# A two-layer decoder trunk (Mamba-2, then sliding-window attention): group 1's transposes one block later, another place for x1, and a last norm that uses TensorE and two store queues

## The chip, the cores and the metric

One core of one Trainium2 chip runs the whole kernel. The metric is the device time of one execution in microseconds (us); the kernel before was timed three times. A profile of one of its executions was taken. Engines: TensorE (PE, matrix products; PEld are its weight loads), VectorE (DVE), ScalarE (ACT), GpSimd (POOL), and SyncE (SP), which here only issues DMAs.

## The reference

The input x has 256 tokens of 2048 numbers, in float32. Two layers follow, each of the form x <- LayerNorm(ALPHA * x + mixer(x)).

The first mixer is a Mamba-2 SSD layer. A projection gives z, xs, B, C and dt. xs, B and C pass a causal convolution of four taps and SiLU. There are 64 heads of width 64 in 8 groups; each group has its own B and C of 128 states. Cut to what matters:

```
zxbcdt = x @ w_in                       # 2048 -> 4096 (z) + 4096 (xs) + 2*1024 (B, C) + 64 (dt)
xbc    = silu(causal_conv(xbc) + conv_b)
y      = ssd(xs * dt, decay(dt * a), B, C) + xs * d_skip
y      = groupwise_rmsnorm(y * silu(z)) * norm_w
x1     = layernorm(ALPHA * x + y @ w_out)
```

The second mixer is grouped-query attention in a window of 128 tokens, with partial rotary positions, a sink per head and a SiLU gate. Keys and values are projected once from x1:

```
kv   = x1 @ kv_w + kv_b
q, g = x1 @ b_w_in                      # 2048 + 2048 columns
o    = softmax_with_sink(rope(q) k^T) v * silu(g)
out  = layernorm(ALPHA * x1 + o @ b_w_out)
```

The layer norm is (x - mean) * rsqrt(var + eps) * g + b, along the 2048 numbers of a token.

## The kernel before

**Precision and weights.** Products run on TensorE in a reduced float32 format. To keep accuracy each operand is split into a high part (a copy, by ACT) and a low part (the difference, by DVE), and three products are added: high*high, high*low, low*high. All weights come from HBM in units of 128 x 2048 float32. `load_unit` (line 101) issues two DMAs of 512 KB on SP's queue into five raw buffers `wr`, has ACT write the high half `wh` (line 112) and DVE the low half `wl` (line 113); there are four `wh` and four `wl` buffers. `next_unit` (line 166) loads two units ahead of their use.

**The first layer.** `group(g)` (line 468) goes through the eight groups. A group consists of ten blocks; a block (`gemm_ws`, line 247) multiplies one unit of weights, stationary, with x, moving (`xH`, `xL`), 48 matmuls of 256 columns (lines 182 to 184). In group 1 and later the blocks are B, C, xs0 to xs3, z0 to z3. The result of an xs block is convolved and passed through SiLU on ACT and DVE (`conv_silu`; the last step is line 322). Later steps of the group are:
- `cb`: products of C and B (lines 390, 391), a mask, and the product with the decay factors `e` (line 395);
- `tr(g, i)`: two transposes of xs_i on TensorE (line 403), and a product with dt on DVE (`xd`, line 408);
- `ymm(g, i)`: the products of `e` and `xd` (line 424) and the skip (line 429);
- `gate(g, i)`: products with z on POOL (lines 436 to 442), a high part on ACT (line 450), a low part on DVE (line 451);
- `norm(g)`: the group's mean square (line 460) and its inverse root on ACT (lines 464, 465).

The out products of group g-1 (`out_unit`, lines 220 to 222, 12 matmuls of 512 columns for each half of the tokens) stand between the blocks of group g. In them y is stationary and the weights move.

**What sets the order.** A table `plan` (built with `at(t, fn, ...)`) says after which block a step is written; t counts blocks, ten to a group. Group 1 has its own entry, with `tr` 4 blocks after the group's start for i = 0, 1; `ymm` for i = 0, 1 and `tr` for i = 2, 3 follow two blocks later, `ymm` for i = 2, 3 four blocks later, and `norm` stands at 10. The framework then places each engine's instructions by its own estimate, so that the order in which an engine gets them is near to the written order but not equal to it.

**Placement in memory.** `xr` holds ALPHA * x and becomes the residual; it lies at the upper end of each partition (16 KiB). Below it, `x1H` and `x1L` (16 KiB each) hold the split output of the first layer; after the last layer's projections are done, the same place holds the tables g and b of the last norm (`gb2`). `x1H` began at byte 180192 of a partition, 480 past a multiple of 512. `xH` begins at 123968 (64 past), `yH`, `yL`, `oH`, `oL`, `wh` and `wl` at multiples of 512.

**The second layer.** For keys, values and queries x1 is stationary and the weights move in 512 columns (`x_stat`, lines 669 to 671: 480 matmuls). For the gate the weights are stationary and x1 moves in 256 columns (lines 182 to 184, called from `gate_block`: 768 matmuls).

**The end.** `out_last` adds the last out products, first all of half 0 of the tokens, then half 1, and takes the statistics of each 512 columns with them (lines 229 and 597). `done2(h)` is the last norm: mean and variance (line 601), the inverse root on ACT (lines 603, 604); then for each of four column ranges t = (x - mean) * g on DVE (line 860). For the ranges in `OFFLOAD` (all four of half 0, ranges 0 and 2 of half 1) ACT multiplies with the inverse root (line 864) and POOL adds b (line 865); for the others DVE does both in one instruction (line 867). SP issues the eight stores (line 868).

Of the kernel before, what the change touches and what calls it, by code (L numbers as in the profile page):

```python
# [8 lines left out]
F32 = mybir.dt.float32  # L9
F32R = mybir.dt.float32r  # L10
I32 = mybir.dt.int32
AF = mybir.ActivationFunctionType
ALU = mybir.AluOpType
AX = mybir.AxisListType

P = 128
S = 256
D = 2048
# [9 lines left out]
TD, TS, CB0, TR0, Y0, CB1 = 5, 5, 8, 9, 10, 5  # L28
# [2 lines left out]
FIRST = [(0, 2), (2, 4), (4, 6), (6, 9), (9, 12), (12, 16)]  # L31
ZPRI = 200
PRE = 1
OFFLOAD = [(0, 1, 2, 3), (0, 2)]
CPRI = 0
OUT_AT = [[], [6, 7, 8, 9]] + [[3, 5, 7, 9]] * 5 + [[7]]

# [22 lines left out]
def trunk(ctx: ExitStack, tc: tile.TileContext, A: dict, out: bass.AP, dbg=None):  # L60
    nc = tc.nc
    PSUM = bass.MemoryType.PSUM

    def pool(name, bufs=1, side=None, space=None, stack=ctx):
        kw = {"space": space} if space is not None else {}
        return stack.enter_context(
            tc.tile_pool(name=name, bufs=bufs, side=side, reuse_waits="tile", **kw)
        )
# [9 lines left out]
    def nm(s):  # L78
        uid[0] += 1
        return f"{s}_{uid[0]}"  # L80
# [4 lines left out]
    def ax_tile():  # L85
        return ax_ps.tile([P, 512], F32, tag="ax", name=nm("ax"), bufs=4)

    cc = cst.tile([P, 896], F32, tag="cc", name="cc")
    ident = cc[:, 0:128]
    ones = cc[:, 128:256]  # L90
# [113 lines left out]


    xp = pool("xp", side="right")
    xr = xp.tile([P, 2, D], F32, tag="xr", name="xr")
    a_stack = ExitStack()
    yp = pool("yp", stack=a_stack)
    w_stack = ExitStack()  # L210
# [330 lines left out]
    def at(t, fn, *a):  # L541
        plan.setdefault(t, []).append((fn, *a))

    at(35, rotary)
    for g in range(NG):
        t = 10 * g
        n = 1 if g == 0 else 0
        if g == 0:
            at(TD, turn_dt, *dts)
            at(TS, sum_decay, 0, 0)  # L550
            at(TS, load_decay, 0, 1)
            at(TS + 1, sum_decay, 0, 1)
            at(TS + 1, exp_decay, 0, 0)
            at(TS + 1, exp_decay, 0, 1)
            pos = dict(cb=CB0, tr=TR0, z=0, norm=Y0 + 5)
        elif g == 1:
            at(Y0, load_decay, 1, 0)
            at(Y0 + 2, sum_decay, 1, 0)
            at(Y0 + 2, load_decay, 1, 1)
            at(Y0 + 4, sum_decay, 1, 1)  # L560
            at(Y0 + 5, exp_decay, 1, 0)
            at(Y0 + 5, exp_decay, 1, 1)
            pos = dict(z=6, cb=CB1, tr=4, norm=10)
        else:
            at(t - 5, load_decay, g, 0)
            at(t - 3, sum_decay, g, 0)
            at(t - 3, load_decay, g, 1)
            at(t - 1, sum_decay, g, 1)
            at(t, exp_decay, g, 0)
            at(t, exp_decay, g, 1)  # L570
            pos = dict(z=6, cb=CB_AT, tr=TR_AT, norm=NORM_AT)
        at(t + pos["cb"], cb, g)

        at(t + pos["tr"], tr, g, 0)
        at(t + pos["tr"], tr, g, 1)
        for k in range(2):
            for i in (2 * k, 2 * k + 1):
                at(t + pos["tr"] + 2 + 2 * k, ymm, g, i)
            if k == 0:
                at(t + pos["tr"] + 2, tr, g, 2)  # L580
                at(t + pos["tr"] + 2, tr, g, 3)
        for i in range(4):
            at(t + max(pos["tr"] + 2 + 2 * (i // 2), pos["z"] + i), gate, g, i)
        at(t + pos["norm"], norm, g)
# [14 lines left out]
    def norm_scale(lp, st, h):  # L599
        mv = lp.tile([P, 2], F32, tag="mv", name=nm("mv"), bufs=2)  # L600
        nc.vector.bn_aggr(mv[:], st[:, h, :, :])
        rs = lp.tile([P, 1], F32, tag="rs", name=nm("rs"), bufs=2)
        nc.scalar.activation(rs[:], mv[:, 1:2], AF.Ln, bias=eps_t[:])
        nc.scalar.activation(rs[:], rs[:], AF.Exp, scale=-0.5)
        return mv, rs
# [35 lines left out]
    bp = pool("bp")  # L641
# [207 lines left out]
    gb2 = [gp.tile([P, D], F32, tag=f"gb{i}", name=f"gb2_{i}") for i in range(2)]  # L849
# [3 lines left out]

    def done2(h):
        mv, rs = norm_scale(bp, st2, h)
        for c in range(4):
            sl = slice(c * 512, (c + 1) * 512)
            v = xr[:, h, sl]
            t = bp.tile([P, 512], F32, tag="pt", name=nm("t"), bufs=4)
            nc.vector.scalar_tensor_tensor(  # L860
                t[:], v, mv[:, 0:1], gb2[0][:, sl], ALU.subtract, ALU.mult
            )
            if c in OFFLOAD[h]:
                nc.scalar.activation(t[:], t[:], AF.Copy, scale=rs[:])
                nc.gpsimd.tensor_tensor(v, t[:], gb2[1][:, sl], ALU.add)
            else:
                nc.vector.scalar_tensor_tensor(v, t[:], rs[:], gb2[1][:, sl], ALU.mult, ALU.add)  # L867
            nc.sync.dma_start(out[h * P : (h + 1) * P, sl], v)

    if PRE:  # L870
        tc.keep_in_program_order(nc.scalar.preload_act_table_set("natural_log_exp_and_others"))
    out_last(*os_[3], None, lambda h, nb: norm_stats(st2, h, nb), done2)


# [87 lines left out]
```

## Time and profile before

| | |
|---|---|
| median of three runs | 1046.5 us (1046.29 to 1047.47) |
| profiled execution, its own time | 1046.29 us |
| span of the profiled execution | 1044.5 us |
| TensorE busy | 1019.1 us, 98% |
| DVE, ACT, POOL busy | 810.5, 518.4, 104.2 us |
| mean granted TensorE clock | 0.992 |
| DMA | 203.50 MB, 195 GB/s on the mean |

How to read the rows: a row of a timeline begins with the start and the duration in us, then the engine, the line of the kernel, the operation, what is written and read, the shape, and the count where neighbours of one kind are merged; a bracket at the end gives the idle time of the engine before the row, and what ended it. A row of a group has the count, the busy time, the mean duration of one in ns and the idle time before them. A row of stretches has the length, the busy time of PE, PEld, DVE, ACT and POOL (with counts), the granted clock, the DMA share and GB/s. Ends of matmuls are modelled, so that a rate is read from one start to the next.

### The profile page before, as it was taken

The numbers are of one execution on the slowest core, as the hardware profiler recorded it, in microseconds if no ns is written. First come the engines' busy times: TensorE is split into PE (matmuls) and PEld (weight loads), VectorE is DVE, ScalarE is ACT, GpSimd is POOL, SyncE is SP. The second block draws the span as 40 slices with busy tenths as digits, with TensorE's granted clock in tenths as the row PEclk, the third lists the DMA queues.
The fourth block names the chain that finished last, engine by engine and source line by source line (L and its number), as shares of the span: only waits on it lengthen the run. The fifth ranks groups of instructions, "written<-read, shape, count | busy, mean of one in ns | idle before, by whom it ended". The sixth has DMA issues, their size and how long they took to land. (4 is left out here: it accounts for less than half of the span.)

```text
span 1044.5 us, 17586 instructions
## 1 busy us (share of the span) xinstructions
PE 1019.1 (98%) x7020; PEld 920.8 (88%) x7020; DVE 810.5 (78%) x1212; ACT 518.4 (50%) x770; POOL 104.2 (10%) x114
## 2 busy tenths in 40 slices
PE   6999899999999999999999999999999999999995
PEld 6999789999999999999999999877887978978974
DVE  5899997876888778787788786698576775775777
ACT  6664545444645544544544464434464544543631
POOL 0001221012003002102102202201000000000003
PEclk9999899999999999999999999999999999999998
DMA  8885586466566655756656555736645455455532
GB/s 277 317 301 198 179 270 226 165 201 215 182 202 226 216 182 195 229 183 208 217 182 207 183 168 176 269 123 224 205 142 172 140 182 165 145 176 179 176 111 80
DMA packets 57170, 203.50 MB, mean 195 GB/s; under 512 B 6448, under 2 KB 8000, under 8 KB 56320
## 3 DMA queue, kind: packets, MB, share of 16 engines
q1 hardware_dynamic: 56016, 196.86, 56.6%
q0 software_dynamic: 1072, 5.53, 1.6%
q8 instruction: 55, 0.90, 0.3%
q14 instruction: 27, 0.22, 0.1%
HBM read 200.13 MB, written 2.23 MB: 194 GB/s over the span
## 5 line engine op out<-in xcount | busy, mean ns | idle before, releaser
L112 ACT ACTIVATE wh<-wr 128x1024 fp32r<-128x1024 f32 x326 | 337.9, 1054 | 324.0 <-PE mm L183 130.1
L113 DVE TENSOR_TENSOR wl<-wr,wh 128x1024 fp32r<-128x1024 f32 x326 | 394.8, 1224 | 103.4 <-ACT wh L112 102.2
L182 PE MATMUL mm<-xH,wh 128*128 128x256 f32 x1296 | 367.9, 284 | 7.2 <-ACT xH L141 6.2
L184 PE MATMUL mm<-xH,wl 128*128 128x256 f32 x1296 | 363.7, 281 | 0.5 <-DVE wl L113 0.4
L183 PE MATMUL mm<-xL,wh 128*128 128x256 f32 x1296 | 363.6, 281 | 0.2 <-DVE xL L142 0.2
L182 PEld LDWEIGHTS mm<-xH,wh 128*128 128x128 f32 x1296 | 245.5, 190 | 10.1 <-ACT xH L141 6.4
L184 PEld LDWEIGHTS mm<-xH,wl 128*128 128x128 f32 x1296 | 245.9, 190 | 0.9 <-DVE wl L113 0.6
L183 PEld LDWEIGHTS mm<-xL,wh 128*128 128x128 f32 x1296 | 245.0, 189 | 1.4 <-DVE xL L142 0.4
L220 PE MATMUL mm<-wh,yH 128*128 128x512 f32 x256 | 101.0, 394 | 0.0
L222 PE MATMUL mm<-wl,yH 128*128 128x512 f32 x256 | 99.9, 390 | 0.0
L221 PE MATMUL mm<-wh,yL 128*128 128x512 f32 x256 | 99.8, 390 | 0.0
L436 POOL TENSOR_TENSOR yz<-yz,z 128x256 f32<-128x256 f32 x32 | 37.3, 1165 | 530.0 <-DVE z L383 469.2
L182 PE MATMUL mm<-x1H,wh 128*128 128x256 f32 x256 | 73.2, 286 | 0.0
L183 PE MATMUL mm<-x1L,wh 128*128 128x256 f32 x256 | 71.9, 281 | 0.0
L184 PE MATMUL mm<-x1H,wl 128*128 128x256 f32 x256 | 71.9, 281 | 0.0
L318 DVE SCALAR_TENSOR_TENSOR cv<-mm,pc,cv 128x255 f32<-128x255 f32 x144 | 68.6, 476 | 1.9 <-ACT cv L316 0.7
L669 PE MATMUL mm<-wh,x1H 128*128 128x512 f32 x160 | 64.1, 400 | 0.0
L671 PE MATMUL mm<-wl,x1H 128*128 128x512 f32 x160 | 63.5, 397 | 0.2
L670 PE MATMUL mm<-wh,x1L 128*128 128x512 f32 x160 | 63.4, 396 | 0.2 <-DVE x1L L633 0.2
L222 PEld LDWEIGHTS mm<-wl,yH 128*128 128x128 f32 x256 | 48.0, 188 | 10.5
L220 PEld LDWEIGHTS mm<-wh,yH 128*128 128x128 f32 x256 | 48.1, 188 | 9.2 <-DVE yz L429 0.2
L221 PEld LDWEIGHTS mm<-wh,yL 128*128 128x128 f32 x256 | 48.1, 188 | 9.1
(173 smaller groups left out, 1316.5 us busy)
## 6 DMA issues: line engine op xcount, KB each, us to landing
wr<-in_wa SPq DMA_DIRECT2D x158, 512.0 KB, 5.0
wr<-in_wo SPq DMA_DIRECT2D x64, 512.0 KB, 4.4
rb<-rscr SPq DMA_DIRECT2D x32, 512.0 KB, 4.7
wr<-in_wq SPq DMA_DIRECT2D x32, 512.0 KB, 4.3
wr<-in_wg SPq DMA_DIRECT2D x32, 512.0 KB, 4.7
wr<-in_wb SPq DMA_DIRECT2D x32, 512.0 KB, 4.3
wr<-in_wkv SPq DMA_DIRECT2D x8, 512.0 KB, 4.9
xr<-in_xk SPq DMA_DIRECT2D x2, 1024.0 KB, 9.7
```

Of the source, the lines that this page charges most:

```text
L112: nc.scalar.activation(hi[:, sl], raws[c][:], AF.Copy)
L113: nc.vector.tensor_tensor(lo[:, sl], raws[c][:], hi[:, sl].bitcast(F32), ALU.subtract)
L182: nc.tensor.matmul(ps, ah, bh, start=first, stop=False)
L183: nc.tensor.matmul(ps, ah, bl, start=False, stop=False)
L184: nc.tensor.matmul(ps, al, bh, start=False, stop=last)
L220: nc.tensor.matmul(ps[:], aH[:, k, hs], u.h[:, ks], start=k == 0, stop=False)
L221: nc.tensor.matmul(ps[:], aL[:, k, hs], u.h[:, ks], start=False, stop=False)
L222: nc.tensor.matmul(ps[:], aH[:, k, hs], u.l[:, ks], start=False, stop=k == 3)
L318: nc.vector.scalar_tensor_tensor(a[:, sft:], ps[:, : S - sft], w(3 - sft), a[:, sft:], ALU.mult, ALU.add)
L669: nc.tensor.matmul(ps[:], x1H[:, kk, hs], u.h[:, ks], start=kk == 0, stop=False)
L670: nc.tensor.matmul(ps[:], x1L[:, kk, hs], u.h[:, ks], start=False, stop=False)
L671: nc.tensor.matmul(ps[:], x1H[:, kk, hs], u.l[:, ks], start=False, stop=kk == KT - 1)
```

## The change

Three things change. In group 1, `tr` and what follows from it, and `norm`, move one block later in the plan. The tile `xr` gets 104 more numbers per partition that nobody uses, so that what lies below it moves down by 416 bytes; `x1H` then begins at byte 179776, 64 past a multiple of 512. The last norm's half 0 does all four ranges with ACT and POOL, as before; half 1 is written anew: for ranges 0 and 1 TensorE first adds b (a product of a row of ones with b) into PSUM, then multiplies t with a diagonal matrix `dg` of the inverse roots, ACT copies the sum out of PSUM and issues the store on its own queue; ranges 2 and 3 are done by DVE and stored by SP. POOL has no part in half 1.

```
-OFFLOAD = [(0, 1, 2, 3), (0, 2)]
...
-    xr = xp.tile([P, 2, D], F32, tag="xr", name="xr")
+    xr = xp.tile([P, 2 * D + 104], F32, tag="xr", name="xr")[:, : 2 * D].rearrange("p (h d) -> p h d", h=2)
...
-            pos = dict(z=6, cb=CB1, tr=4, norm=10)
+            pos = dict(z=6, cb=CB1, tr=5, norm=11)
...
     def done2(h):
         mv, rs = norm_scale(bp, st2, h)
+        if h:
+            dg = bp.tile([P, P], F32, tag="dg", name="dg")
+            pss = [ax_tile(), ax_tile()]
+            for c in range(2):
+                sl = slice(c * 512, (c + 1) * 512)
+                nc.tensor.matmul(pss[c][:], ones[0:1, :], gb2[1][0:1, sl], start=True, stop=False)
+            nc.scalar.activation(dg[:], ident, AF.Copy, scale=rs[:])
+            for c in range(4):
+                sl = slice(c * 512, (c + 1) * 512)
+                v = xr[:, h, sl]
+                o = out[h * P : (h + 1) * P, sl]
+                t = bp.tile([P, 512], F32, tag="pt", name=nm("t"), bufs=4)
+                nc.vector.scalar_tensor_tensor(
+                    t[:], v, mv[:, 0:1], gb2[0][:, sl], ALU.subtract, ALU.mult
+                )
+                if c < 2:
+                    nc.tensor.matmul(pss[c][:], dg[:], t[:], start=False, stop=True)
+                    nc.scalar.copy(v, pss[c][:])
+                    nc.scalar.dma_start(o, v)
+                else:
+                    nc.vector.scalar_tensor_tensor(v, t[:], rs[:], gb2[1][:, sl], ALU.mult, ALU.add)
+                    nc.sync.dma_start(o, v)
+            return
         for c in range(4):
...
-            if c in OFFLOAD[h]:
-                nc.scalar.activation(t[:], t[:], AF.Copy, scale=rs[:])
-                nc.gpsimd.tensor_tensor(v, t[:], gb2[1][:, sl], ALU.add)
-            else:
-                nc.vector.scalar_tensor_tensor(v, t[:], rs[:], gb2[1][:, sl], ALU.mult, ALU.add)
+            nc.scalar.activation(t[:], t[:], AF.Copy, scale=rs[:])
+            nc.gpsimd.tensor_tensor(v, t[:], gb2[1][:, sl], ALU.add)
             nc.sync.dma_start(out[h * P : (h + 1) * P, sl], v)
```

## The prediction

> **What bounds the kernel now.** I read the page first, then what TensorE waited for, then the timelines around the one place where it waits, around the passes that read x1, and at the end.
>
> ```profile
> span 1044.5 us, 17586 instructions
> PE 1019.1 (98%) x7020; PEld 920.8 (88%) x7020; DVE 810.5 (78%) x1212; ACT 518.4 (50%) x770; POOL 104.2 (10%) x114
> ...
> PE ax L403 <- DVE xs L322: 4.7, 1, 4.7
> ...
> 107.71:112.40 4.69, 0.00 (x0) 0.03 (x1) 4.37 (x6) 3.16 (x6) 4.18 (x5) 0.80 0.54 176
> 112.40:117.32 4.92, 4.92 (x23) 4.92 (x24) 4.92 (x14) 1.72 (x3) 0.00 (x0) 0.50 0.56 175
> ```
>
> TensorE is busy for 98% of the span, so the kernel gets shorter only where TensorE stands idle, runs slowly, or has finished. The third line is its longest wait after the start: one transpose of x (line 403), 4.7 us. The last two lines are stretches: length, busy time of PE, weight loads, DVE, ACT and POOL, granted clock, DMA share, GB/s. After the idle 4.69 us TensorE works 4.92 us at clock 0.50.
>
> **Part 1: the transposes of group 1.** The idle time and its surroundings, TensorE first, then what it needed:
>
> ```profile
> 107.33 0.38 PE L403 MATMUL ax<-cc,xs 128*128 128x128 f32 x2
> 120.51 0.50 PE L460 MATMUL ax<-cc,sq 128*128 128x1 f32 x4
> 121.53 0.36 PE L182 MATMUL mm<-xH,wh 128*128 128x256 f32 x1
> 121.73 0.28 PE L183 MATMUL mm<-xL,wh 128*128 128x256 f32 x1
> 124.91 0.28 PE L183 MATMUL mm<-xL,wh 128*128 128x256 f32 x1
> ...
> 102.33 2.34 DVE L113 TENSOR_TENSOR wl<-wr,wh 128x1024 fp32r<-128x1024 f32 x2
> 111.31 0.94 DVE L322 SCALAR_TENSOR_TENSOR xs<-xs,cv 128x256 f32<-128x256 f32 x1
> 116.85 0.74 DVE L408 TENSOR_TENSOR xd<-ax,dtx 128x256 f32<-128x256 f32 x2
> 117.52 1.21 DVE L113 TENSOR_TENSOR wl<-wr,wh 128x1024 fp32r<-128x1024 f32 x1
> 121.81 0.56 DVE L392 TENSOR_TENSOR cbm<-ax,cc 128x384 f32<-128x384 f32 x1 [1.61 <-PE ax L391]
> 122.67 1.75 DVE L395 TENSOR_TENSOR e<-e,cbm 128x1536 f32<-128x1536 f32 x1
> 126.39 0.48 DVE L318 SCALAR_TENSOR_TENSOR cv<-mm,pc,cv 128x253 f32<-128x253 f32 x1
> 112.33 1.04 ACT L112 ACTIVATE wh<-wr 128x1024 fp32r<-128x1024 f32 x1
> 117.97 0.40 ACT L321 ACTIVATE xs<-cv 128x256 f32<-128x256 f32 x1
> ...
> 121.53:145.96 24.43, 24.43 (x168) 21.80 (x167) 23.50 (x35) 14.06 (x19) 4.84 (x5) 1.00 0.61 198
> ```
>
> From 107.33 to 121.53 TensorE does four transposes, the block xs3 (48 matmuls), the norm's two products and the C·B products: 14.20 us. At full speed a matmul of such a block takes (124.91 - 121.73) / 27 = 0.1178 us (27 steps between the two rows), so the block takes 5.65; line 460 to the next block is 1.02; the four records of the transposes together some 0.35, as the first two last 0.38 with their drain. That is 7.0, so the stall costs 7.2: 4.7 idle, the rest at half clock, where 23 matmuls take 4.92 us.
>
> In the changed kernel the order on TensorE is: xs3 at once (DVE splits its weights in the row of 102.33), norm, C·B, then the two transposes, then z0. The transposes come up at 107.33 + 5.65 + 1.02 = 114.0; xs1, which they wait for, is written at 111.31 + 0.94 = 112.25, by instructions that do not wait for TensorE. Nothing waits, the clock has no reason to fall, and z0 starts at 114.4 instead of 121.5.
>
> What is late next? The weights of z1, two blocks on. DVE is busy without a break from 116.85; the order there is now: two splits of the out weights, xs2, cbm, cv, L395, cv, L395, cv, two xd, then the first split for z1. By the rows: a split 1.21; xs2 some 0.4; cbm and cv 0.86 (121.81 to 122.67); L395, cv, L395 3.72 (122.67 to 126.39); cv 0.39; the xd pair 0.67 (116.85 to 117.52). 116.85 + 2.42 + 0.4 + 0.86 + 3.72 + 0.39 + 0.67 + 1.21 = 126.5, a little less where neighbours overlap; the 1.61 us in which DVE waited for TensorE at L392 are gone, as C·B comes 7 us earlier. ACT's half for z1 is done at 113.4 and its xs2 at 118.4, both in time. TensorE reaches z1 after z0 (5.8 with its start) and 24 out matmuls (0.227 each, part 2) at 125.7, and its third matmul needs the split: a wait of 0.4.
>
> Moved with it: the products ymm of i = 0, 1 and the transposes of i = 2, 3 now stand behind z1, their inputs written by 126; ymm of i = 2, 3 behind z3; POOL's gating and ACT's and DVE's yH and yL follow them, and the norm goes one block into group 2. What reads all this, the out products of group 1, starts in block 3 of group 2. On SP's queue the weight loads keep their order, and the decay loads of group 2 are passed by two to four of them; rb is read several blocks later. The last row of the fence shows TensorE busy throughout the 24 us behind the stall, with ACT at 14 and DVE at 23.5: DVE has little left, yet none of its later splits is due before TensorE gets to it, as each stands a block or more ahead. I carry the 0.4 and nothing else: **-6.8 us**. Ends: 0 (the wait moves whole to z1) and -7.2.
>
> **Part 2: x1 at 64 past a multiple of 512.** The padding of xr (104 floats) moves all that is placed below it: in the built program x1H goes from byte 180192 (480 past a multiple of 512, 32 past one of 64) to 179776 (64 past 512), x1L likewise. Who reads x1, and how fast:
>
> ```profile
> L669 PE MATMUL mm<-wh,x1H 128*128 128x512 f32 x160 | 64.1, 400 | 0.0
> ...
> 716.39 0.39 PE L669 MATMUL mm<-wh,x1H 128*128 128x512 f32 x1
> 732.49 0.40 PE L669 MATMUL mm<-wh,x1H 128*128 128x512 f32 x1
> 1015.16 0.39 PE L220 MATMUL mm<-wh,oH 128*128 128x512 f32 x1
> 1024.68 0.39 PE L220 MATMUL mm<-wh,oH 128*128 128x512 f32 x1
> ...
> L182 PE MATMUL mm<-x1H,wh 128*128 128x256 f32 x256 | 73.2, 286 | 0.0
> 752.88 0.28 PE L182 MATMUL mm<-x1H,wh 128*128 128x256 f32 x1
> 757.85 0.28 PE L182 MATMUL mm<-x1H,wh 128*128 128x256 f32 x1
> ```
>
> Lines 669 to 671 hold x1 stationary, 3 x 160 matmuls. Between the two rows of L669 are 69 steps: 16.10 / 69 = 233.3 ns each. The out products (line 220) have the same shape, moving weights and order of operands, but a stationary o that begins at a multiple of 512: 42 steps, 9.52 / 42 = 226.7 ns. 6.6 ns x 480 = 3.2 us. In the gate blocks x1 is the moving operand, 3 x 256 matmuls: 4.97 / 42 = 118.3 ns, against 117.8 above, where xH begins at 64 past 512: 0.5 x 768 = 0.4 us. No row has a 128-column stationary at 64 past 512 in this kind of stream, so the ends are 0 and -3.6, and above 0 by as much, as no row excludes it. I take the gain whole, since the one neighbour that lies at 64, xH, steps without the extra: **-3.6 us**. What DVE, ACT and the DMAs do on xr and on the last norm's tables, which move too, I carry at 0: no row compares them, and they lie beside TensorE's work but for the last 8 us.
>
> The Trainium skill ("Advanced Engine Details and Errata", section Memory Cachelines) speaks against this part: SBUF lines are 16 bytes and what counts is that accesses stay in a line. Both addresses are multiples of 16, so by it the move is worth 0 and the sum is 3.6 higher. The 6.6 ns above are not explained by it, which is why I do not follow it.
>
> **Part 3: the last norm.** Half 0 is as before. Half 1 after the last matmul:
>
> ```profile
> 1032.61 0.39 PE L222 MATMUL mm<-wl,oH 128*128 128x512 f32 x1
> 1034.86 2.08 DVE L860 SCALAR_TENSOR_TENSOR t<-xr,mv,gb 128x512 f32<-128x512 f32 x3
> 1035.11 0.20 ACT L604 ACTIVATE rs<-rs 128x1 f32<-128x1 f32 x1
> 1036.50 3.22 POOL L865 TENSOR_TENSOR xr<-t,gb 128x512 f32<-128x512 f32 x2 [2.44 <-ACT t L864]
> 1038.52 1.75 DVE L860 SCALAR_TENSOR_TENSOR t<-xr,mv,gb 128x512 f32<-128x512 f32 x1
> 1040.30 0.75 DVE L867 SCALAR_TENSOR_TENSOR xr<-t,rs,gb 128x512 f32<-128x512 f32 x1
> ...
> out<-xr SPq DMA_DIRECT2D x8, 256.0 KB, 2.3
> 1035.00:1036.00 1.00, 0.00 (x0) 0.00 (x0) 1.00 (x2) 0.58 (x3) 0.00 (x0) 0.75 0.63 236
> 1039.00:1040.00 1.00, 0.00 (x0) 0.00 (x0) 1.00 (x1) 0.00 (x0) 0.72 (x1) 0.50 1.03 383
> ...
> L809 PE MATMUL ax<-pt,vt 128*64 128x512 f32 x48 | 12.1, 609 | 0.0
> ```
>
> While POOL adds, DVE's L860 takes 1.75 instead of 0.69 (2.08 / 3). Removed on the path: POOL's two adds, ACT's two scalings, one L867. Now DVE does four t to 34.86 + 2.77 = 37.6 and two L867 to 38.35 and 39.05; the last store leaves SP at 39.1 where it left at 41.05 (1040.30 + 0.75): -2.0. Beside it: the two one-row bias products run when TensorE falls idle at 33.0, until about 34.7 at worst; dg on ACT until 35.65; each float32 product is two records, by L809 1.0 to 1.2 us, so products end at 36.7 and 37.6, ACT copies (0.72 each) and its two stores leave at 37.5 and 38.65 (a store's issue is queued between the copies). The row of 1035 to 1036 shows the clock falling to 0.50 some 2.5 us after TensorE stopped; should that hit both products, ACT's last store leaves at about 40.2. Stores then crowd: at the 383 GB/s seen, a store of 256 KB needs 0.7 us, three of them between 39.0 and 41.15, where one alone would be through at 40.6. Ends: -2.0, and -0.8 for the slow clock; I take **-1.5**.
>
> The Trainium skill ("DMA: Bandwidth & Descriptors", section Issuing engines are not separate DMA queues) says that a second issuing queue saves issue time alone; by it the ACT queue is worth nothing here and the term is that of the earlier data.
>
> **The sum.** The profiled execution took 1046.29 us, with a span of 1044.5 and 1.8 around it; it is the fastest of the three, 0.2 under the median. 1046.29 - 6.8 - 3.6 - 1.5 = 1034.4; for a median 1034.6.
>
> **The rivals.** *x1's offset is worth nothing.*
>
> ```profile
> L403 PE MATMUL ax<-cc,xs 128*128 128x128 f32 x64 | 11.0, 285 | 4.7 <-DVE xs L322 4.7
> L627 PE MATMUL ax<-cc,xr 128*128 128x128 f32 x32 | 4.9, 276 | 0.3 <-DVE xr L622 0.3
> ```
>
> For it: transposes of an xs that begins at 64 past 512 and of an xr at 480 past take alike, 285 and 276 ns. Against it: the 6.6 ns between lines 669 and 220. It gives 1034.6 + 3.6 = 1038.2.
>
> *The wait moves to z1.* For it: DVE's 23.5 of 24.4 us. In the stretch from 107.71 the mean clock is 0.80, so it fell after some 2.8 us of idleness; a wait of that length at z1 brings the half clock back too. Whole, that returns 6.8: 1041.4. Against it: the walk above, and that TensorE now waits for no split behind the stall.
>
> *Slower: 64 past 512 is a worse place than 480 for a stationary operand.* The price is 480 times the difference; parts 1 and 3 bring 8.3, so it decides from 8.3 / 480 = 17 ns over the present 233, at 251 ns a step. For it: no row shows this place in such a stream. Against it: at that place xH is the quicker moving operand. At 255 ns, without the gain of part 2: 1046.5 - 8.3 + 480 x 0.0217 = 1048.6.
>
> **How the numbers follow.** The forecast 0.62, with a range of its own of 1033.3 to 1036.0 (part 3 at its ends, and a wait at z1 of 0 to 1 us); x1 worth nothing 0.20; the wait at z1, whole or in part, 0.09; slower 0.05; the rest, between, 0.04. The range for 8 in 10 runs from 1033.3 past the second case to 1039.0. A measurement of this kernel tells some 0.2% (2 us) from no change; faster 0.93, same 0.02, slower 0.05.
>
> **What would show it.** Part 1: no wait at line 403, clock 1.00 from 100 to 130, z0 starting near 114.4; wrong if a wait for wl of over 1 us stands at z1. Part 2: steps of 227 ns at the lines that were 669 to 671, and 117.8 in the gate blocks; wrong if 233 stays. Part 3: four t of 0.69 each, the last store issued 6.4 us after the last out matmul instead of 8.4; wrong if the records of the two products are twice as long and ACT's store is the last.

## The result and the profile after

| | before | after |
|---|---|---|
| median of six runs each | 1046.45 us (1046.03 to 1047.70) | 1040.34 us (1038.65 to 1041.36) |
| ratio of times, 95% interval | | 0.9927 (0.9917 to 0.9938) |
| profiled execution, its own time | 1046.29 us | 1039.01 us |
| span of the profiled execution | 1044.5 us | 1037.2 us |

The changed kernel is 6.1 us faster by the two medians and 7.6 us (6.5 to 8.7) by the recorded ratio, which is not the ratio of the medians; 11.9 were forecast. Its runs also lie wider apart, 2.7 us against 1.7. The head of the page, and from the list of what TensorE waited for, after:

```profile
span 1037.2 us, 17602 instructions
PE 1020.7 (98%) x7028; PEld 919.9 (89%) x7028; DVE 809.5 (78%) x1212; ACT 518.1 (50%) x771; POOL 99.7 (10%) x112
```

```profile
PE ax L403 <- DVE xs L322: 0.9, 1, 0.9
PE ax L873 <- ACT dg L863: 0.9, 1, 0.9
...
PE mm L183 <- DVE wl L112: 0.5, 1, 0.5
PE ax L390 <- DVE ct L322: 0.5, 1, 0.5
```

The wait of 4.7 us is gone. Two new rows belong together: line 403 for 0.9 and line 390 for 0.5, both in group 3 (after 265 us). The row of line 183 is at the start of the kernel. The place where the stall was, after (stretches, then TensorE):

```profile
107.33:114.17 6.84, 6.84 (x60) 6.79 (x59) 6.59 (x13) 3.82 (x6) 3.98 (x5) 1.00 0.63 200
114.17:138.60 24.43, 24.43 (x167) 21.73 (x166) 23.66 (x32) 14.41 (x18) 1.49 (x1) 1.00 0.69 230
```

```profile
112.72 0.50 PE L460 MATMUL ax<-cc,sq 128*128 128x1 f32 x4
113.82 0.60 PE L403 MATMUL ax<-cc,xs 128*128 128x128 f32 x4
114.17 0.36 PE L181 MATMUL mm<-xH,wh 128*128 128x256 f32 x1
125.38 0.28 PE L181 MATMUL mm<-xH,wh 128*128 128x256 f32 x1
125.49 0.28 PE L182 MATMUL mm<-xL,wh 128*128 128x256 f32 x1
125.77 0.39 PE L183 MATMUL mm<-xH,wl 128*128 128x256 f32 x1
```

TensorE is busy throughout at clock 1.00, z0 starts at 114.17 (121.53 before), and z1 at 125.38 has its third product 0.28 us behind the second instead of 0.12.

To see where the rest went I cut TensorE's time at the starts of six matmuls that every version has. This table is worked out from the records of the traces, one execution each; the columns are: from the span's start to the 41st product of xH and wh; on to block xs2 of group 1; to xs2 of group 2 (holds part 1); to z0 of group 3; to the first matmul with x1 stationary; to the last out matmul (holds what reads x1); to the span's end (holds the last norm).

```
                     start    xs2,g1   xs2,g2   z0,g3    x1       last mm  end
before               26.40    75.16    97.51   101.08   395.36   337.11    11.91
part 1 alone         28.92    76.12    91.09   102.02   395.36   337.11    11.89
part 2 alone         27.20    75.70    98.20   100.89   395.36   336.52    11.91
part 3 alone         27.36    76.12    97.53   103.13   395.35   337.12    10.74
before, early loads  25.38    75.90    97.42   100.91   395.41   337.12    11.91
after                25.61    75.70    90.63   102.69   395.36   336.58    10.68
after, again         26.90    75.70    91.91   101.67   395.37   336.35    11.29
after, one queue     26.12    75.70    91.87   100.89   395.36   336.55    10.76
after, early loads   27.00    75.90    91.69   100.91   395.41   336.55    11.36
  and x1 at 0        25.78    75.90    90.39   100.91   395.40   335.69    10.65
  and x1 at 256      26.97    75.90    90.39   100.91   395.41   335.66    11.35
  and x1 at 128      25.60    75.56    92.23   100.91   395.41   337.16    11.35
  256, identity      27.64    75.90    91.09   100.91   395.39   335.66    10.64
  256, filler        25.62    76.56    92.06   100.91   395.41   335.65    10.66
```

Between the first profiles of before and after: -0.8 and +0.5 ahead of the change, -6.9 in the stretch of part 1, +1.6 in group 3, -0.5 where x1 is read, -1.2 at the end; together -7.3, the difference of the spans. So the gain of part 2 is missing, and 1.6 us of part 1 came back 155 us behind the stall. The experiments take these up; names in the table are those of the runs below.

### The profile page after: what moved, and what is told of

Same layout as the page of the kernel before. It is cut to its first block, busy times and chain, and to the rows that moved or that the text cites. A ratio compares the mean times of both kernels' runs of the same rounds, so it can differ in the third digit from the quotient of the medians.

```text
span 1037.2 us, 17602 instructions
## 1 busy us (share of the span) xinstructions
PE 1020.7 (98%) x7028; PEld 919.9 (89%) x7028; DVE 809.5 (78%) x1212; ACT 518.1 (50%) x771; POOL 99.7 (10%) x112
## 5 line engine op out<-in xcount | busy, mean ns | idle before, releaser
L112 DVE TENSOR_TENSOR wl<-wr,wh 128x1024 fp32r<-128x1024 f32 x326 | 393.9, 1222 | 98.9 <-ACT wh L111 97.7
L220 PE MATMUL mm<-wh,yH 128*128 128x512 f32 x256 | 100.9, 394 | 0.0
```

The lines of the kernel that those rows point to most:

```text
L112: nc.vector.tensor_tensor(lo[:, sl], raws[c][:], hi[:, sl].bitcast(F32), ALU.subtract)
L220: nc.tensor.matmul(ps[:], aH[:, k, hs], u.h[:, ks], start=k == 0, stop=False)
```

## The experiments

### Each part alone, and the changed kernel once more

Part 1 alone is the one line `pos = dict(z=6, cb=CB1, tr=5, norm=11)`; part 2 alone the padding of `xr`; part 3 alone the new `done2`, without the other two.

> Part 1 alone (group 1's transposes and norm one block later). In the trace of the changed kernel TensorE is 7.1 us ahead of the kernel before from 165 to 260 us, and then only 5.5: at the start of group 3 VectorE stands 6.6 us (5.0 before) at line 522 until the small load posi of GpSimd's queue has landed, and TensorE waits 0.5 us at line 390 and 0.9 us at line 403. Theory 1 (the load's landing decides): the gain is 7.1 us where posi lands in some 5 us and falls by what it takes longer; so 5.5 to 7.1 us faster. Theory 2 (VectorE is behind with its splits, as it lost the 7 us in which it caught up): always 5.5 us faster, whatever posi takes. My forecast of 6.8 would stand in both only if the wait in group 3 stays away.

> Part 2 alone (x1 at 64 past a multiple of 512 instead of 480 past). By the trace of the changed kernel only the gate blocks gain: 768 matmuls, 0.6 us in all, and the 480 matmuls with x1 stationary stay at 233 ns: 0.6 us faster. The forecast had 3.6 us faster, 227 ns at the 480 matmuls. A gain of 3 us or more here, with 233 ns standing, would mean that the place acts somewhere else.

> Part 3 alone (half 1 of the last norm with TensorE and two store queues). From the last matmul of the out products to the end of the span it is 11.9 us in the kernel before and 10.6 us in the changed kernel, so 1.3 us faster; the forecast had 1.5, with ends of 0.8 and 2.0. If the three parts alone add up to less than the whole gain by over 1 us, they work on each other, which the traces do not show so far.

> The changed kernel once more, for a second profile. Its first six runs lie between 1038.7 and 1041.4 us, more widely than those of the kernel before. Theory 1: what differs from run to run is how long posi takes to land at the start of group 3; a profile of a run near 1040.5 shows a wait at line 522 that is longer than 6.6 us, and a TensorE wait in group 3 that is longer than the 1.6 us of the first profile, perhaps with a stretch at half clock behind it (the mean clock of these runs is 0.996 to 0.997, against 0.999 in the profiled one). Theory 2: the wait at 522 is the same, and the difference lies in another place, at the start or the end.

| | median | ratio to the kernel before (1047.54, 23 runs) |
|---|---|---|
| part 1 alone | 1040.75 us | 0.9939 (0.9925 to 0.9952) |
| part 2 alone | 1046.53 us | 0.9991 (0.9981 to 1.0001) |
| part 3 alone | 1047.27 us | 0.9994 (0.9985 to 1.0003) |
| all three, again | 1040.41 us | 0.9932 (0.9917 to 0.9946) |

By these ratios part 1 carries 6.4 of the 7.1 us. Parts 2 and 3 alone (0.9 and 0.6 us by the ratios) cannot be told from nothing by their times; the table of stretches shows their 0.6 and 1.2 us. Some 8 us of the three against 7.1 for all together lies within the intervals: there is no sign that the parts work on each other.

What came back in group 3 hangs on one small load. GpSimd issues `posi` (1 KB), VectorE converts it at line 522, and all that VectorE has queued stands behind that. Line 522 before and after (with the row of `ct`, for which line 390 waits); the load's landing with part 1 alone and with part 3 alone, and there TensorE's wait:

```profile
260.29 0.17 DVE L522 CAST posf<-posi 128x2 f32<-128x2 int32 x1 [4.99 <-DMA posi<-in_pos]
```

```profile
254.78 0.17 DVE L522 CAST posf<-posi 128x2 f32<-128x2 int32 x1 [6.60 <-DMA posi<-in_pos]
...
269.53 0.43 DVE L322 SCALAR_TENSOR_TENSOR ct<-ct,cv 128x256 f32<-128x256 f32 x1 [0.50 <-ACT ct L321]
```

```profile
DMA to landing us min/median/max: 6.0/6.0/6.0
```

```profile
DMA to landing us min/median/max: 7.3/7.3/7.3
```

```profile
PE ax L390 <- DVE ct L322: 1.1, 1, 1.1
```

VectorE stood 6.60 us after, 4.99 before. The stretch to z0 of group 3 is 100.9 to 101.1 us where the load landed in 4.5 (one queue), 4.8 or 5.1 us, 101.7 at 5.7, and 102.0, 102.7 and 103.1 where it took 6.0, 6.7 and 7.3. Part 3 alone keeps the stall in group 1 and loses 2 us all the same, so theory 2 (VectorE late because it lost its time to catch up) falls: the loss follows the landing, in kernels of both kinds.

In its second profile the changed kernel's load landed in 5.7 us and cost 0.7; that run's excess lay at z1 as well, which the forecast had at 0.4:

```profile
126.84 0.28 PE L182 MATMUL mm<-xL,wh 128*128 128x256 f32 x1
128.35 0.39 PE L183 MATMUL mm<-xH,wl 128*128 128x256 f32 x1 [1.23 <-DVE wl L112]
```

Over the ten profiles with part 1 its stretch takes 90.4 to 92.2 us, 91.3 on the mean, against 97.4 to 98.2 (97.7) in four without it: 6.3 us. The spread comes from z1, whose third product is 0 to 1.5 us late in the ten, and the traces show where from. VectorE's last wait before the split that this product needs is at line 451, for the high part of a gated output of group 0 (line 450, ACT); from there to the end of that split it works 17.0 to 17.3 us without a break in all ten. Where this work begins 6.2 us or more before z0, nothing is late; at 5.8 to 5.2 us it is 0.2 to 0.6, at 4.7 to 4.2 it is 1.2 to 1.5. Why group 0's gating comes earlier or later was not followed up. The first column scatters too, 25.4 to 28.9, and there the clock differs: between 20 and 25 us, after and part 1 alone:

```profile
20.00:25.00 5.00, 4.49 (x38) 4.28 (x37) 3.03 (x6) 4.43 (x8) 0.00 (x0) 1.00 0.98 379
```

```profile
20.00:25.00 5.00, 4.29 (x20) 4.30 (x21) 2.27 (x5) 3.08 (x6) 0.00 (x0) 0.50 0.94 373
```

At half clock 20 matmuls are done in place of 38. In seven of the fourteen profiles the clock falls like this at about 20 us, for 3.4 us in six of them and for 6.8 in part 1 alone; their first column is 26.9 to 28.9 us, that of the other seven 25.4 to 26.4. So neither theory on the spread of the runs holds alone: the start, the load and z1 each add up to a few microseconds, and two of the three have nothing to do with the change.

### The small loads ten blocks earlier

```
+    pos0 = ap.tile([P, 2], I32, tag="pos0", name="pos0")
+    inv0 = ap.tile([P, 8], F32, tag="inv0", name="inv0")
+    def rotary_load():
+        tc.keep_in_program_order(nc.gpsimd.dma_start(pos0[:], A["pos"]))
+        tc.keep_in_program_order(nc.gpsimd.dma_start(inv0[:], A["inv"]))
...
-        tc.keep_in_program_order(nc.gpsimd.dma_start(posi[:], A["pos"]))
+        tc.keep_in_program_order(nc.gpsimd.tensor_copy(posi[:], pos0[:]))
...
+    at(25, rotary_load)
     at(35, rotary)
```

> The changed kernel, with the two small loads of positions and inverse frequencies issued ten blocks earlier on GpSimd's queue into tiles of their own; at the old place GpSimd copies them. Where the loads stood, VectorE waited for posi 5.0 to 7.2 us in the profiles so far, and TensorE's time from the middle of group 2 to the middle of group 3 was 101.1, 100.9, 101.7, 102.0, 102.7 and 103.1 us at landings of 5.1, 4.8, 5.7, 6.0, 6.7 and 7.3 us after the issue. Theory 1 (that landing takes the time back): no wait at lines 390 and 403 in group 3, 101.0 us for this stretch, and a median 0.7 to 1.7 us under the changed kernel's. Theory 2 (VectorE is behind with splits): the waits stay, the stretch keeps over 101.5 us, and the time stays.

> The same edit on the kernel before. Theory 1: the landing is a wait of both kernels, not one that part 1 made; the stretch takes 101.0 us here too and the median falls by 0.5 to 2 us. Rival: the kernel before has enough slack behind its stall in group 1, so it does not gain.

Line 522 is line 529 here. The framework also moved that line and what hangs on it ahead of two splits on VectorE; on TensorE and SP nothing moved. The changed kernel with early loads:

```profile
250.95 0.17 DVE L529 CAST posf<-posi 128x2 f32<-128x2 int32 x1 [0.77 <-POOL posi L525]
```

The stretch takes 100.9 us in all seven profiles with this edit, and the waits at lines 390 and 403 are gone: theory 1 holds for the wait. The five runs lie between 1039.37 and 1040.64 us (1.3 us apart; the twelve of the changed kernel were 4.2 apart), the median is 1039.48, 0.9927 (0.9915 to 0.9940) of the kernel before. The median is 0.9 us under the changed kernel's, but the ratio is the one of its first six runs, so the times do not settle the expected gain of 0.7 to 1.7 us. On the kernel before the edit gives 1046.95 us, 0.9996 (0.9987 to 1.0004): the 0.5 to 2 us expected of it are not to be seen in the time.

### One store queue

```
-                    nc.scalar.dma_start(o, v)
+                    nc.sync.dma_start(o, v)
```

> The changed kernel with all four stores of half 1 issued by SP. If the second queue is worth nothing, from the last out matmul to the end stays at 10.7 to 11.3 us. If it is worth something, the stores of the TensorE ranges stand in one line with the others; as each issue takes SP some 0.35 to 0.5 us and the four leave within 1.4 us of each other in the changed kernel, no more than 0.5 us is lost.

The time is 1039.91 us, 0.9929 (0.9916 to 0.9943), and the last stretch takes 10.76 us against 10.68 in the first profile of the changed kernel. By these two profiles the second queue is worth 0.1 us here. Stores of half 1 after, the stretch in which they land, and the stores with one queue:

```profile
1031.54 0.37 ACTq L875 DMA_DIRECT2D out<-xr  x1
1032.57 0.34 ACTq L875 DMA_DIRECT2D out<-xr  x1
...
1032.24 0.99 SPq L878 DMA_DIRECT2D out<-xr  x2
```

```profile
1033.00:1034.00 1.00, 0.00 (x0) 0.00 (x0) 0.00 (x0) 0.00 (x0) 0.00 (x0) 1.00 1.04 381
```

```profile
1031.45 1.19 SPq L875 DMA_DIRECT2D out<-xr  x2
1032.73 0.91 SPq L878 DMA_DIRECT2D out<-xr  x2
```

All four have been issued by 1033.2 after and by 1033.6 with one queue, and after, the DMA engines then move 381 GB/s, what the stores of the kernel before reached (383). The Trainium skill ("DMA: Bandwidth & Descriptors", section Issuing engines are not separate DMA queues) says that issuing from several engines saves issue time only; these rows agree.

### Where x1 begins

The padding of `xr` alone changes: 120, 56 and 88 numbers put x1 at 0, 256 and 128 past a multiple of 512. All with the early loads.

> As the run with the early loads, and x1 begins at a multiple of 512 (120 numbers of padding instead of 104), like the stationary operands of the out products, which step at 227 ns. Theory A (the place within 512 bytes decides, but 64 is as bad as 480): 227 ns at the 480 matmuls with x1 stationary, 3.2 us less than the run with the early loads. Theory B (the place within 512 bytes has nothing to do with it): 233 ns, and no change but for the gate blocks, which may go back by 0.6 us.

> As the run with the early loads, with x1 at 256 past a multiple of 512 (56 numbers of padding). So far the 480 matmuls with x1 stationary step at 233 ns with x1 at 480 and 64 past, and at 227 with x1 at 0; the 768 gate matmuls at 118.3, 117.5 and 120 ns. Theory A1 (a stationary block of 512 bytes per partition must not cross a multiple of 512): 233 ns here too. Theory A2 (a multiple of 128 or 256 is enough): 227 ns. For the gate no theory: 117.5 to 120 ns, worth 2 us between the ends. With 227 and 117.5 it would be 3 us faster than the run with the early loads.

> As before it, with x1 at 128 past a multiple of 512 (88 numbers of padding). Theory A1: 233 ns at the 480 matmuls with x1 stationary. Theory A2: 227 ns if a multiple of 128 is enough, 233 if it takes 256. Gate 117.5 to 120 ns.

The same two matmuls with x1 stationary, 69 steps apart, and the same two of a gate block, 42 steps apart, at 64 (after), 0, 256 and 128 past:

```profile
710.90 0.39 PE L669 MATMUL mm<-wh,x1H 128*128 128x512 f32 x1
726.99 0.40 PE L669 MATMUL mm<-wh,x1H 128*128 128x512 f32 x1
747.35 0.28 PE L181 MATMUL mm<-x1H,wh 128*128 128x256 f32 x1
752.29 0.28 PE L181 MATMUL mm<-x1H,wh 128*128 128x256 f32 x1
```

```profile
709.26 0.39 PE L677 MATMUL mm<-wh,x1H 128*128 128x512 f32 x1
724.93 0.39 PE L677 MATMUL mm<-wh,x1H 128*128 128x512 f32 x1
745.06 0.28 PE L181 MATMUL mm<-x1H,wh 128*128 128x256 f32 x1
750.09 0.28 PE L181 MATMUL mm<-x1H,wh 128*128 128x256 f32 x1
```

```profile
710.45 0.39 PE L677 MATMUL mm<-wh,x1H 128*128 128x512 f32 x1
726.11 0.39 PE L677 MATMUL mm<-wh,x1H 128*128 128x512 f32 x1
746.25 0.28 PE L181 MATMUL mm<-x1H,wh 128*128 128x256 f32 x1
751.28 0.28 PE L181 MATMUL mm<-x1H,wh 128*128 128x256 f32 x1
```

```profile
710.60 0.39 PE L677 MATMUL mm<-wh,x1H 128*128 128x512 f32 x1
726.63 0.39 PE L677 MATMUL mm<-wh,x1H 128*128 128x512 f32 x1
747.04 0.27 PE L181 MATMUL mm<-x1H,wh 128*128 128x256 f32 x1
752.01 0.28 PE L181 MATMUL mm<-x1H,wh 128*128 128x256 f32 x1
```

Differences divided by the steps, with the kernel before (480 past) from the prediction:

| x1 past a multiple of 512 | 0 | 64 | 128 | 256 | 480 |
|---|---|---|---|---|---|
| ns a step, x1 stationary | 227 | 233 | 232 | 227 | 233 |
| ns a step, x1 moving (gate) | 119.8 | 117.6 | 118.3 | 119.8 | 118.3 |
| stretch to the last matmul, us | 335.7 | 336.5 | 337.2 | 335.7 | 337.1 |

A stationary x1 is quick at 0 and at 256: theory B falls, and so does A1, since at 256 every block of 512 bytes crosses a multiple of 512. A2 holds with 256: of the five places the multiples of 256 are quick and the others are not. A moving x1 wants the opposite: 64 is the best of the five and 0 and 256 are the worst. The two effects pull against each other, 480 x 6 ns against 768 x 2.2 ns, and of the 3 us only 0.9 is left between 64 and 256. The medians are 1038.55 us at 0, 0.9925 (0.9912 to 0.9939); 1038.19 us at 256, 0.9906 (0.9889 to 0.9922); 1040.41 us at 128, 0.9932 (0.9917 to 0.9947). By the stretches, 0 and 256 are the same version; their times differ by no more than runs do. 256 with early loads has the lowest median of all versions here, and is 2.2 us under the changed kernel's; its interval still touches that of the changed kernel beside it (0.9917 to 0.9946).

### The clock in the last norm

Two products of the new norm take 1.98 us in some profiles and up to 3.78 in others. The TensorE rows after and in the changed kernel's second profile, and there the granted clock:

```profile
1029.76 1.98 PE L873 MATMUL ax<-t,dg 128*128 128x512 f32 x4 [0.89 <-ACT dg L863]
```

```profile
1031.10 3.53 PE L873 MATMUL ax<-t,dg 128*128 128x512 f32 x4 [0.89 <-ACT dg L863]
```

```profile
1029.00:1031.00 2.00, 1.21 (x3) 0.18 (x1) 1.83 (x5) 0.85 (x3) 0.34 (x1) 1.00 0.67 256
1031.00:1033.00 2.00, 1.90 (x3) 0.92 (x4) 2.00 (x4) 0.09 (x2) 0.00 (x0) 0.60 0.00 0
1033.00:1035.00 2.00, 1.63 (x2) 0.06 (x1) 1.22 (x2) 0.88 (x2) 0.00 (x0) 0.55 0.28 109
```

The last stretch is 10.7 us with the full clock and 11.3 with the half. Two versions of the best kernel tried to keep the clock up: b enters by all 128 rows (identity times table), and then, besides, three products that nobody reads run in the wait for `dg`.

```
-                nc.tensor.matmul(pss[c][:], ones[0:1, :], gb2[1][0:1, sl], start=True, stop=False)
+                nc.tensor.matmul(pss[c][:], ident, gb2[1][:, sl], start=True, stop=False)
...
+            oH = os_[3][0]
+            warm = ax_tile()
+            for i in range(3):
+                nc.tensor.matmul(warm[:], oH[:, 0, :P], oH[:, 0:2, :], start=True, stop=True)
```

> The version so far best (early loads, x1 at 256 past 512), and the two products that put b into PSUM use all 128 rows (identity times the table of b) instead of one row. In the eight profiles with the new norm the products of t and dg took 0.53 to 0.43 us a record in four (TensorE 1.98 us for them in all) and up to 1.06 us in the other four, as the granted clock fell to 0.50 some 2 to 4 us after the last out product; the stretch from that product to the end was 10.7 us in the first case and 11.3 in the second (with one between). Theory 1 (a product of one row counts for the clock as if TensorE stood idle): with 128 rows the clock stays at 1.00 until the stores, and the stretch is 10.7 us. Theory 2 (the 0.9 us of waiting for dg, or the mixture, is what counts): the clock falls as before in some executions, and the stretch is 11.3 us where it does.

> As the run before it, and three products of 512 columns whose result nobody reads stand between the products of b and those of t, in the 0.9 us in which TensorE waits for dg. Under both theories the clock stays at 1.00 and the stretch from the last out product to the end is 10.7 us; if it falls all the same, the clock is decided by what lies further back, or by how the stretch meets windows that run by themselves. Time: 0 to 0.6 us under the run at 256 past, whose median was 1038.2.

Both show 1.98 us for the products, and 10.64 and 10.66 us for the last stretch; the medians are 1038.84 us, 0.9919 (0.9906 to 0.9931), and 1038.64 us, 0.9915 (0.9899 to 0.9930), not under that of the version they start from. In the eight profiles with the one-row products the clock stayed up for both products in three and for half of them in a fourth (2.77 us, part 3 alone; the expectation counts it with the first). By that count, two profiles with the full clock would come by chance about one time in seven. The clock records of the traces (start and length of each stretch at one clock) settle more.

In all fourteen, every stretch from the first rise of the clock to its last fall lasts a whole number of 3.413 us, from 1 to 301 of them, and the first rise comes 7.8 to 11.5 us after the span's start, at another time in each profile. So the clock changes at the edges of windows that run by themselves, and the same tail meets them at other places: in the same kernel, the changed one, the clock fell 3.5 us after the start of the last out matmul in one profile and 8.2 us after it in the other. The Trainium skill ("TensorE: Matmul & The Clock Gate", section Part 1: The HAM clock gate) says that the window of activity is free-running, so that the point of change varies from run to run; these records agree.

Part 3 alone and the first of the two versions meet the windows alike: an edge lies 4.26 and 4.30 us after the start of the last out matmul. The window before that edge and the one behind it, part 3 alone (one row), then 128 rows:

```profile
1037.46:1040.87 3.41, 2.52 (x7) 0.96 (x6) 3.24 (x7) 0.90 (x3) 0.58 (x1) 1.00 0.41 154
1040.87:1044.20 3.33, 1.70 (x3) 0.13 (x1) 2.05 (x4) 1.17 (x2) 0.00 (x0) 0.50 0.54 196
```

```profile
1027.49:1030.90 3.41, 2.33 (x6) 0.81 (x5) 3.24 (x7) 0.90 (x3) 0.53 (x1) 1.00 0.40 154
1030.90:1034.32 3.42, 0.88 (x3) 0.05 (x1) 2.01 (x4) 1.17 (x2) 0.00 (x0) 1.00 0.56 205
```

TensorE was busy for 2.52 us of the window with one row and for 2.33 with 128, and the clock fell behind the first alone. With x1 at 256 (one row) it fell even behind a window of which TensorE was busy for 3.26 us of 3.41. Counted without the one-row products, the windows of this tail part cleanly: in the five profiles of the eight in which the clock fell during the products of t or ahead of them, the window before held 0.54 to 1.28 us of products of 128 rows; in the three others, every window that ended within 6 us of the start of the last out matmul held 1.56 us or more. So theory 1 fits all ten profiles: for the clock, a product of one row counted as next to nothing. The wait for `dg`, theory 2, is 0.9 us in all eight, and 1.1 us in the profile with 128 rows, which kept the clock; but each of the two versions has one profile only. In time the two versions gain nothing that the runs show.

## Why the prediction was half right

**Part 1, right in mechanism, 0.5 us too high.** Forecast -6.8, measured -6.3 on the mean of the profiles (-6.9 in the first). z0 starts at 114.17 for 114.4, the clock stays up, nothing waits at line 403 in group 1. The mis-sized term is the wait for z1, put at 0.4 us: the third product comes 0.2 us late in the first profile, 1.4 in the second and 0.8 on the mean of the ten. TensorE waits there for over 1 us, the sign named against this part, in five of the ten. The walk was sound on the mean: it put the end of the split that z1 needs 12.1 us behind the start of z0, and that is the mean of the ten, which lie between 10.8 and 12.8. The rival "the wait moves to z1" came about by a part of its size at most.

**Part 2, the step that failed.** Forecast -3.6, measured -0.6. The 0.4 for the gate came (118.3 to 117.6 ns, the whole stretch -0.6), the 3.2 for the stationary x1 did not: 233 ns stayed, which the prediction had named as the sign against itself. The failing step is the choice "I take the gain whole, since the one neighbour that lies at 64, xH, steps without the extra". xH is a moving operand; the table above shows that moving and stationary operands like opposite places. The comparison of 233 with 227 was sound, and its cause is indeed the place of x1: 227 appears at 0, where o lies. Only 64 is not such a place. So the rival "x1's offset is worth nothing" was right on the main term, for a reason that it did not have. The Trainium skill ("Advanced Engine Details and Errata", section Memory Cachelines) speaks of 16-byte lines, by which the move was worth nothing; 128 and 256 past are both multiples of 16 and differ by 5 ns a step, so the measurement goes beyond that rule.

**Part 3, right in mechanism, 0.3 to 0.9 us too high.** Forecast -1.5, with -0.8 as the end for a slow clock; measured -1.2 with the full clock and -0.6 with the half, -0.9 on the mean of eight profiles. The four t took 0.69 us each, and the two last results were written 6.3 us after the last out matmul began, for the 6.4 forecast of the last store:

```profile
1026.57 0.39 PE L222 MATMUL mm<-wl,oH 128*128 128x512 f32 x1
...
1028.81 2.74 DVE L869 SCALAR_TENSOR_TENSOR t<-xr,mv,gb 128x512 f32<-128x512 f32 x4
1031.47 1.41 DVE L877 SCALAR_TENSOR_TENSOR xr<-t,rs,gb 128x512 f32<-128x512 f32 x2
```

The slow clock was weighed as an end only; it was there for both products in four of the eight, and in these ACT's store left last, the sign named against this part. The crowd of the stores was seen but counted too low: measured from the start of the last out matmul, the last store left SP at 6.3 us instead of 8.5 and landed at 9.6 instead of 10.8, so that 0.9 us was lost in the crowd where the prediction had some 0.5 (41.15 against 40.6).

**The sum.** With the measured sizes, 6.3 + 0.6 + 0.9 = 7.8 us. Against 1046.45 that is 1038.7. The median of the six runs, 1040.34, lies above the range, whose upper end of 1039.0 stopped behind the second case; by the recorded ratio, 0.9927, the time is 1038.8, inside the range by 0.2. That it is inside by this measure is owed to the second case, x1 worth nothing at a chance of 0.20, and not to the forecast. Measured beside 23 runs of the kernel before, the gain was 7.1 us. What is left between 7.8 and these measures is of the size by which the runs of these kernels move: the start scatters by 3.5 us, the load of `posi` by 2 and the stretch of z1 by 1.8; it is not assigned more closely than this. The forecast was made against one execution in which that load had cost almost nothing (5.1 us to landing), and a range from one profile had no room for it.

## What to carry to other kernels

Before a gain is carried over from a neighbour, look whether the neighbour plays the same part: here a moving operand's good place said nothing of a stationary one's, and at the five places tried a tile read in both ways had no place that was best for both. After a stall is removed, look for waits whose length is a transfer's latency, however small the transfer: an engine that works in order and waits for one keeps all that is queued behind it. A single profile is one draw; the start, small loads and the clock at the end moved this kernel by more than two of the three edits.

## What was not expected of the hardware

- A load of 1 KB issued by GpSimd took between 4.5 and 7.3 us to land in the middle of the kernel, where a load of 512 KB on SP's queue took 5.1 us on the median (after, the list of DMA issues: count, size, median time to landing):

```profile
wr<-in_wa SPq DMA_DIRECT2D x158, 512.0 KB, 5.1
```

- With a stationary operand of 128 x 128 float32 and 512 moving columns, matmuls stepped at 227 ns where it began at 0 or 256 past a multiple of 512, and at 232 to 233 at 64, 128 and 480; as the moving operand of 256 columns the same tile stepped at 117.6 ns at 64, 118.3 at 128 and 480, and 119.8 at 0 and 256.
- With the new norm and its one-row products the clock fell 2.5 to 4.3 us after the start of the last out matmul in five profiles, and 8.2 to 9.0 us after it in three. It changed at the edges of windows of 3.413 us, and one-row products did not hold it up: it fell behind a window of which they and others kept TensorE busy for 3.26 us.
